# A diffusion trunk in split precision: high and low value features of one neighbourhood head side by side in one product, and new duration estimates for the planner

## The chip, the cores and the metric

The kernel runs on one core of one Trainium2 chip. The metric is the device time of one execution in microseconds (us). Before the change three runs took 1600.81, 1604.31 and 1604.71 us; the median is 1604.31 us.

Engine names are those of the profile: PE is TensorE (PEld its weight loads), DVE is VectorE, ACT is ScalarE, POOL is GpSimd, SP is SyncE, which issues the DMAs.

## The reference

The program is a backbone of two layers over 256 latent tokens and 256 context tokens, width 1024, all in float32. Each layer has four branches side by side, merged by gates, then an MLP with squared ReLU. Cut to what matters here:

```python
u = x * (1.0 + sc1) + sh1
p = split_proj(u @ w_in[l] + b_in[l])            # all branches' inputs and the gates
y_a, y_b = local_branches(p, ...)                # short gated conv | Conformer conv (31 taps, LayerNorm, silu)
y_c = diff_post(diff_latent(q_d, k_d, v_d, k_dc, v_dc, lam), ...)   # differential attention, 4 heads
y_d = na_latent(q_n, k_n, v_n, k_nc, v_nc, rpb)  # neighbourhood attention, 8 heads of 64 features
y = merge_out(p[I_GATE], (y_a, y_b, y_c, y_d), w_branch[l], b_branch[l], w_o[l])
x = layer_norm(ALPHA * x + g1 * y, ...)
x = layer_norm(ALPHA * x + g2 * sq_relu_ffn(x * (1.0 + sc2) + sh2, w_ff1[l], w_ff2[l]), ...)
```

A neighbourhood head is `softmax(q k^T + bias) v`, with 64 features for q, k and v. The latent tokens attend to all 512 tokens, the context tokens (layer 0 alone) to the 256 of the context. In layer 1 the context gives keys and values and nothing else.

## The kernel before

**Precision.** Matrices are multiplied in a rounded float32 format. To keep the accuracy, each operand is split in a high part (rounded by a copy on ACT) and a low part (the rest, a subtraction on DVE). A product of two such operands is three products on PE: high x high, high x low, low x high (`mm3`). The low x low term is left out.

**Weights.** All weights stream through in units of 128 x 1024 numbers (512 KB), in a fixed order: SP loads `raw`, ACT makes `whi`, DVE makes `wlo`, each with three buffers, and PE uses them. In layer 0 a unit of the projections is 24 products over 512 columns (latent and context tokens), in layer 1 mostly 24 over 256 columns.

**Order of a layer.** `main` issues, one after the other: the Conformer branch's inputs, differential attention's first half, the short conv, the second half, merge 0, the first half of the neighbourhood heads (`na_stage` 0), merge 2, the second half (`na_stage` 1), merge 1, merge 3, the output projection, the MLP. Merge i multiplies branch i's output (`ya`, `yb`, `yc`, `yd` for i = 0 to 3) by its weights (tile `br`) and applies the gates; it starts when all four tiles of that branch are there. `yb` comes from the Conformer branch: 31 taps per channel tile on DVE (tile `conf`), then a normalisation over the channels (`mu`, `var`, `rs`), then the splits into `yb`. `yd` comes from the neighbourhood heads.

**A neighbourhood head.** Four or two score tiles `S` on PE, the bias, maximum, exponential and division on DVE and ACT (tile `P`), transposes on PE (`PT`), the split into `pt`, and the products with the values in `na_head` and `pv` (lines 1252 to 1260 and 1289 to 1313). The values of the branch lie in four pairs of tiles, high and low, each 128 keys x 512 features. `pv` takes 128 features, those of two heads, as the stationary operand and 256 queries as the moving one, with three products per 128 keys; the head then reads only its own 64 rows of the PSUM tile `o`. Layer 0 has 6 key tiles per head (4 for the latent, 2 for the context queries) and layer 1 has 4. The 64 rows are split straight from PSUM into `yd`. Differential heads use `pv` with all 128 rows.

**What sets the order.** Each engine's queue is written by a planner in the program (`Sched`). Threads (one per tile, head, weight stream) yield operations with an estimated duration; at each step the planner takes the operation that could start first by these estimates, and among equals the one with the lowest priority number (weights 3, norm 8, projections' evacuation 10 to 12, modulation sums 12, heads 15, softmax 16, `main`'s products 50, taps 90). The estimates thus decide only the order on each engine, buffers' turns and DMA issues included; on the chip the engines wait for one another by semaphores. `gemm` and `score_mm` count a product as its columns at 0.4167 ns plus 2 ns, ACT's operations cost 95 ns plus 0.833 ns per element, 93 more for a per-partition scale, a bias and an accumulator each.

Of the kernel before, what the change touches and what calls it, by code (L numbers as in the profile page):

```python
# [9 lines left out]
F32 = mybir.dt.float32  # L10
F32R = mybir.dt.float32r
AF = mybir.ActivationFunctionType
ALU = mybir.AluOpType
# [12 lines left out]
FIRST = 5  # L26
ADA_PACE = 108
TO_PE = 300.0
PRIO_ADA = 27
PRIO_X = 60  # L30
COLD = 6800.0
# [16 lines left out]
KD = D // 128  # L48
# [101 lines left out]
class Sched:  # L150
    @staticmethod
    def lat(a, b):
# [5 lines left out]
        if "PE" in (a, b):  # L158
            return 200.0 if a == "PE" else TO_PE
        return 205.0 if "POOL" in (a, b) else 143.0  # L160
# [138 lines left out]
def size(ap):  # L299
    n = 1  # L300
    for s in ap.shape[1:]:
        n *= s
    return n


class Kernel(Sched):
# [49 lines left out]
    def act(self, out, in_, func, scale=1.0, bias=None, accum=None):  # L356
        nc, a = self.nc, self._a
        kw = {}
        if bias is not None:
            kw["bias"] = a(bias)  # L360
        if accum is not None:
            kw["accum_out"] = a(accum)
        if isinstance(scale, V) or scale != 1.0:
            kw["scale"] = a(scale)
        cost = 95 + 0.833 * size(out.ap) + 93 * (isinstance(scale, V) + isinstance(bias, V)) + 93 * (accum is not None)
        return self._op("ACT", cost,
                        lambda: nc.scalar.activation(out=out.ap, in_=in_.ap, func=func, **kw),  # L367
                        [out] + ([accum] if accum is not None else []), [in_, scale, bias],
                        table=None if func in (AF.Copy, AF.Identity) else int(func == AF.Ln))
# [60 lines left out]
    def gemm(self, out, pairs, cost, first=True, last=True):  # L430

        n = len(pairs)
        step = max(1, int(1300 // (3 * cost)))
        for i in range(0, n, step):
            calls, r = [], []
            for j in range(i, min(n, i + step)):
                a, b = pairs[j]
                calls += self.mm3(out, a, b, first and j == 0, last and j == n - 1)
                r += [a[0], a[1], b[0], b[1]]
            yield self.mm(calls, [out], r, (cost + 2) * len(calls))  # L440

    def wide(self, l, name, nb, which, tiles, a, ws, done):

# [368 lines left out]
    def ada_all(self):  # L812
# [3 lines left out]
        for g in (1, 2):  # L816
            yield from self.ada(0, g, n)
            n += 16
        self.spawn(self.ada_next(), PRIO_ADA)

# [121 lines left out]
    def first_unit(self, i, n):  # L942
        w = yield self.wait("w", i)
        w = Weight(w, 128)
        p = yield self.alloc("ps", "first", name="mm")
        for k in range(KD):
            for s in range(2):
                yield self.wait("uk", 0, 0, s, k // 2)
            a, b = w(k), self.ucut(0, 0, k, 0, n)
            yield self.mm(self.mm3(p[:, 0:n], a, b, k == 0, k == KD - 1), [p], [*a, *b], 3 * (0.4167 * n + 2))  # L950
        self.release(*w.views())
        self.signal("first", i, val=p)

# [188 lines left out]
        yield from self.wide(l, (br,), 0, range(4), range(4), self.u[l, 0], [], done)  # L1142

    def value_split(self, l, br, t, ps, vs, left, uses):
        vb = yield self.wait("vb", l, br)
        f = yield self.s("att", F32, "vf")
        yield self.tt(f, ps, vb, ALU.add)
        self.release(ps)
        yield from self.split(f, *vs[t])
        self.release(f)  # L1150
        left[0] -= 1
        if not left[0]:
            self.release(vb)
            self.shared((br, l), [x for p in vs for x in p], uses)
# [9 lines left out]
    def score_mm(self, S, q, k, m, q0, k0, nk):  # L1164
        qs, ks = slice(q0, q0 + 128), slice(k0, k0 + nk)
        return self.mm([(S.ap, q[m].ap[:, qs], k[m].ap[:, ks], True, False, {}),
                        (S.ap, q[2 + m].ap[:, qs], k[m].ap[:, ks], False, True, {})],
                       [S], [q[m], q[2 + m], k[m]], 2 * (0.4167 * nk + 2))

    def softmax(self, S, sb, nk, p, stv, i):  # L1170
        nc = self.nc
# [80 lines left out]
    def pv(self, o, vs, c0, pts, s):  # L1252
# [6 lines left out]
                          self.cut(pts[kt // 2], (slice(None), slice((kt % 2) * 256, (kt % 2) * 256 + 256)))))  # L1259
        return self.gemm(o, pairs, 107)  # L1260

    def diff_head(self, l, st, j, n):
        h = 2 * st + j
        pts = []
        for s in range(n // 256):
            p = yield from self.p_parts(l, "d", h, s)
            pts.append(p)
        vs = yield self.wait("dv", l)
        o = yield self.alloc("ps", "att", name="o")
        for s in range(n // 256):  # L1270
            yield from self.pv(o[:, s * 256:s * 256 + 256], vs, h * 128, pts[s], s)
            for p in pts[s]:
                self.release(*p)
        self.done("dv", l)
        sq = yield self.s("tmp", F32, "osq")
        yield self.act(sq[:, 0:n], o[:, 0:n], AF.Square)
        ms = yield self.alloc("ps", "att", name="ms")
        yield self.ones_mm(ms[:, 0:n], self.on128, sq[:, 0:n], True, True)
        r = yield from self.rsqrt(ms[:, 0:n], n)
        self.release(ms)  # L1280
        f = sq[:, 0:n]
        yield self.tt(f, o[:, 0:n], r[:, 0:n], ALU.mult)
        self.release(o, r)
        y = yield from self.pair("y", "yc")
        yield from self.split(f, y[0][:, 0:n], y[1][:, 0:n], self.gd[l])
        self.release(sq)
        self.signal("y", l, 2, h, val=y)

    def na_head(self, l, st, h, n):
        j, e = (h % 4) // 2, h % 2  # L1290
        rows = slice(64 * e, 64 * e + 64)
        pts = []
        for s in range(n // 256):
            p = yield from self.p_parts(l, "n", h, s)
            pts.append(p)
        vs = yield self.wait("nv", l)
        o = yield self.alloc("ps", "att", name="o")
        for s in range(n // 256):
            yield from self.pv(o[:, s * 256:s * 256 + 256], vs, (2 * st + j) * 128, pts[s], s)
            for p in pts[s]:  # L1300
                self.release(*p)
        self.done("nv", l)
        key = ("yd", l, st, j)
        if key not in self.uses:
            self.uses[key] = 0
            y = yield from self.pair("y", "yd")
            self.signal("ydt", l, st, j, val=y)
        y = yield self.wait("ydt", l, st, j)
        yield from self.split(o[rows, 0:n], y[0][rows, 0:n], y[1][rows, 0:n])
        self.release(o)  # L1310
        self.uses[key] += 1
        if self.uses[key] == 2:
            self.signal("y", l, 3, 2 * st + j, val=y)
# [260 lines left out]
    def ff1_rows(self, l, ms, n):  # L1574

        ps, ws = [], []
        for m in ms:
            w = yield from self.weight(l, "f1", m)
            p = yield self.alloc("ps", "main", name="mm")
            ps.append(p)  # L1580
            ws.append(w)
        for k in range(KD):
            yield self.wait("uk", l, 1, 0, k // 2)
            for p, w in zip(ps, ws):
                a, b = w(k), self.ucut(l, 1, k, 0, n)
                yield self.mm(self.mm3(p[:, 0:n], a, b, k == 0, k == KD - 1), [p], [*a, *b], 3 * (0.4167 * n + 2))
        for m, p, w in zip(ms, ps, ws):
            self.release(*w.views())
            self.spawn(self.ff1_evac(l, m, n, p), 10)
# [294 lines left out]
```

## Time and profile before

| | |
|---|---|
| median of three runs | 1604.31 us |
| the profiled execution | 1606.23 us |
| its span, first to last instruction | 1604.5 us |
| granted TensorE clock, mean | 0.994 of full speed |
| PE, PEld busy | 98%, 84% |
| DVE, ACT busy | 80%, 55% |
| mean of the DMA traffic | 158 GB/s |

A row of a group reads: line, engine, operation, tile written <- tiles read, shape written <- shape read, count, then busy us, mean ns of one, and the idle time of the engine ahead of these operations with what ended it. Rows of one engine can overlap, since operations are pipelined: the price of one in a full queue is the distance between two starts. Line 421 is the helper that issues all matrix products, 374 the two-operand operations of DVE, 367 those of ACT, 401 DVE's with a scalar and a tensor; so rows are told apart by their tiles.

### The profile page before, as it was taken

To read this page: it belongs to the slowest core of one execution; us is meant where nothing else is said; L and a number is where in the kernel's file an instruction comes from. 1 tells how busy PE (TensorE), PEld (TensorE's weight loads), DVE (VectorE), ACT (ScalarE), POOL (GpSimd) and SP (SyncE) were. 2 spreads that over 40 slices of the span, in tenths; PEclk is the share of its full clock that TensorE was granted. 3 is DMA by queue.
4 is the path that set the end of the run, shared out by engine and by line. 5 is a ranking of instruction groups with operands and counts; after the bars stand their busy time and mean duration, and the time that the engine had idled before them with its cause. 6 is when DMAs were issued, how large, how long until landed. Compare 5 with 4: busy or idle time off the path is not lost. (4 is left out here: it accounts for less than half of the span.)

```text
span 1604.5 us, 23073 instructions
## 1 busy us (share of the span) xinstructions
PE 1571.9 (98%) x8768; PEld 1349.3 (84%) x8768; DVE 1290.1 (80%) x2156; ACT 883.2 (55%) x1413; POOL 12.0 (1%) x51
## 2 busy tenths in 40 slices
PE   7999999999999999999999999999999989999997
PEld 4888888888888888887887878989998989989997
DVE  3899999699999647986777786999999886774566
ACT  3476376455745544642424334776686585476553
POOL 0000000000000000000000000000000000000000
PEclk9999999999999999999999999999999999999999
DMA  9322322454465155455655644533443335745563
GB/s 373 104 77 79 105 79 79 162 171 160 145 195 160 67 170 197 142 193 177 198 194 192 214 152 141 200 129 136 154 148 116 138 118 176 245 140 189 194 223 108
DMA packets 80707, 254.30 MB, mean 158 GB/s; under 512 B 9028, under 2 KB 13892, under 8 KB 80596
## 3 DMA queue, kind: packets, MB, share of 16 engines
q1 hardware_dynamic: 80596, 252.84, 46.3%
q8 instruction: 68, 1.11, 0.3%
q14 instruction: 43, 0.35, 0.1%
HBM read 250.67 MB, written 2.13 MB: 158 GB/s over the span
## 5 line engine op out<-in xcount | busy, mean ns | idle before, releaser
L421 PE MATMUL mm<-u,whi 128*128 128x512 f32 (+1 forms) x3168 | 786.7, 339 | 1.5 <-DVE u L374 1.0
L421 PEld LDWEIGHTS mm<-u,whi 128*128 128x128 f32 x3168 | 544.9, 190 | 67.7 <-DVE u L374 2.9
L374 DVE TENSOR_TENSOR wlo<-raw,whi 128x1024 fp32r<-128x1024 f32 x335 | 408.5, 1221 | 159.4 <-PE mm L421 70.2
L421 PE MATMUL mm<-u,wlo 128*128 128x512 f32 (+1 forms) x1584 | 534.5, 337 | 0.4 <-DVE wlo L374 0.4
L367 ACT ACTIVATE whi<-raw 128x1024 fp32r<-128x1024 f32 x335 | 353.8, 1057 | 306.5 <-DVE wlo L374 117.6
L421 PEld LDWEIGHTS mm<-u,wlo 128*128 128x128 f32 x1584 | 301.4, 190 | 32.3 <-DVE wlo L374 0.6
L421 PE MATMUL f<-whi,a 128*128 128x512 f32 (+1 forms) x760 | 235.3, 388 | 0.0
L401 DVE SCALAR_TENSOR_TENSOR sums<-araw,cs,sums 128x512 f32<-128x512 f32 x280 | 196.7, 744 | 39.7 <-DMA araw<-in_w_ada 39.4
L421 PEld LDWEIGHTS f<-whi,a 128*128 128x128 f32 x760 | 142.3, 188 | 29.5 <-issue 0.8
L421 PE MATMUL f<-wlo,a 128*128 128x512 f32 (+1 forms) x380 | 147.2, 387 | 0.0
L401 DVE SCALAR_TENSOR_TENSOR conf<-glu,sm,conf 128x512 f32<-128x512 f32 (+1 forms) x240 | 139.0, 611 | 1.1
L421 PEld LDWEIGHTS f<-wlo,a 128*128 128x128 f32 x380 | 71.4, 188 | 14.5 <-DVE wlo L374 0.2
L367 ACT ACTIVATE P<-S,st 128x512 f32<-128x512 f32 (+1 forms) x96 | 58.4, 612 | 11.2 <-DVE st L1173 10.5
L367 ACT ACTIVATE gth<-mm,hb 128x512 f32<-128x512 f32 (+1 forms) x64 | 36.9, 577 | 42.5 <-PE mm L421 42.2
L421 PE MATMUL wo<-whi,mg 128*128 128x512 f32 (+1 forms) x184 | 56.3, 382 | 0.0
L1173 DVE TENSOR_REDUCE st<-S 128x1 f32<-128x512 f32 (+1 forms) x96 | 55.2, 590 | 0.8 <-PE S L421 0.6
L367 ACT ACTIVATE qk<-ra 64x512 fp32r<-64x512 f32 (+1 forms) x72 | 41.5, 576 | 18.5 <-DVE ra L374 17.2
L367 ACT ACTIVATE bh<-br,hb 128x512 f32<-128x512 f32 (+1 forms) x64 | 36.4, 573 | 27.0 <-PE br L421 26.9
L367 ACT ACTIVATE a2f<-mm 128x512 f32<-128x512 f32 (+1 forms) x64 | 30.8, 482 | 33.1 <-PE mm L421 33.0
L421 PE MATMUL S<-qk 128*128 128x512 f32 (+1 forms) x192 | 47.8, 369 | 1.0 <-ACT P L367 0.7
L421 PE MATMUL o<-pt,v 128*128 128x256 f32 x360 | 47.3, 285 | 0.1
L421 PEld LDWEIGHTS o<-pt,v 128*128 128x128 f32 x360 | 45.4, 191 | 1.6 <-issue 0.5
(204 smaller groups left out, 1901.1 us busy)
## 6 DMA issues: line engine op xcount, KB each, us to landing
raw<-in_W SPq DMA_DIRECT2D x344, 512.0 KB
araw<-in_w_ada SPq DMA_DIRECT2D x80, 512.0 KB
a<-in_w_ada SPq DMA_DIRECT2D x32, 256.0 KB
bt<-in_rpb SPq DMA_DIRECT2D x32, 128.0 KB
row<-g SPq DMA_DIRECT2D x12, 256.0 KB
x<-in_x_t SPq DMA_DIRECT2D x8, 256.0 KB
row<-in_ln_g SPq DMA_DIRECT2D x8, 256.0 KB
row<-in_ln_b SPq DMA_DIRECT2D x8, 256.0 KB
```

The lines of the kernel that those rows point to most:

```text
L367: lambda: nc.scalar.activation(out=out.ap, in_=in_.ap, func=func, **kw),
L374: return self._op(eng, cost, lambda: e.tensor_tensor(out=out.ap, in0=x.ap, in1=y.ap, op=op), [out], [x, y])
L401: return self._op("DVE", cost, lambda: nc.vector.scalar_tensor_tensor(out=out.ap, in0=x.ap, scalar=a(s), in1=y.ap, op0=op0, op1=op1), [out ...
L421: nc.tensor.matmul(out=out, lhsT=x, rhs=y, start=start, stop=stop, **kw)
L1173: yield self.dve(68 + 1.04 * nk, lambda: nc.vector.tensor_reduce(out=mx.ap, in_=S.ap, axis=AX.X, op=ALU.max, negate=True), [mx], [S])
```

## The change

Three things:

1. `value_split` writes the values of the neighbourhood branch in another layout: a tile's 512 columns hold, for each of four heads, 64 high features and 64 low ones. Each value tile is split in two halves of 256 features for that.
2. `na_head` uses a new `pv_head`: the stationary operand is one head's 64 high and 64 low features, and it is multiplied by the high and by the low part of the probabilities, two products per 128 keys. Rows 0 to 63 of `o` then hold the high features' part and rows 64 to 127 the low ones'. ACT copies rows 64 to 127 of `o` into a temporary, DVE adds rows 0 to 63, and the sum is split into `yd`. The low x low term is now in the sum.
3. The planner's estimates: a product is its columns plus `MM` = 13.3 ns; an ACT operation with a per-partition scale or bias costs 65 ns more, once; one that writes 64 partitions costs 13 ns plus 0.23 ns per element more.

```diff
+MM = 13.3
@@ act
-        cost = 95 + 0.833 * size(out.ap) + 93 * (isinstance(scale, V) + isinstance(bias, V)) + 93 * (accum is not None)
+        n = size(out.ap)
+        cost = 95 + 0.833 * n + 93 * (accum is not None)
+        if out.ap.shape[0] == 64:
+            cost += 13 + 0.23 * n
+        elif isinstance(scale, V) or isinstance(bias, V):
+            cost += 65
@@ gemm (and in the same way first_unit, score_mm, ff1_rows)
-            yield self.mm(calls, [out], r, (cost + 2) * len(calls))
+            yield self.mm(calls, [out], r, (cost + MM) * len(calls))
@@ value_split
-        yield from self.split(f, *vs[t])
+        if br == "dv":
+            yield from self.split(f, *vs[t])
+        else:
+            for g in range(2):
+                x = f[:, g * 256:g * 256 + 256].re("p (h d) -> p h d", h=4)
+                o = vs[t][g].re("p (h c d) -> p h c d", h=4, c=2)
+                yield from self.split(x, o[:, :, 0, :], o[:, :, 1, :])
@@ new
+    def pv_head(self, o, v, pts, s, c0):
+        n = 2 * len(pts)
+        for kt in range(n):
+            x = v[2 * (kt + 2 * s)][:, c0:c0 + 128]
+            cols = slice((kt % 2) * 256, (kt % 2) * 256 + 256)
+            ps = [p[:, cols] for p in pts[kt // 2]]
+            yield self.mm([(o.ap, x.ap, p.ap, kt == 0 and i == 0, kt == n - 1 and i == 1, {}) for i, p in enumerate(ps)],
+                          [o], [x, *ps], 2 * (107 + MM))
@@ na_head
-            yield from self.pv(o[:, s * 256:s * 256 + 256], vs, (2 * st + j) * 128, pts[s], s)
+            yield from self.pv_head(o[:, s * 256:s * 256 + 256], vs[st:], pts[s], s, (2 * j + e) * 128)
...
+        t = yield self.s("tmp", F32, "olo")
+        yield self.act(t[0:64, 0:n], o[64:128, 0:n], AF.Copy)
+        f = t[rows, 0:n]
+        yield self.tt(f, o[0:64, 0:n], t[0:64, 0:n], ALU.add)
+        self.release(o)
...
-        yield from self.split(o[rows, 0:n], y[0][rows, 0:n], y[1][rows, 0:n])
-        self.release(o)
+        yield from self.split(f, y[0][rows, 0:n], y[1][rows, 0:n])
+        self.release(t)
```

More of the change, by code (lines that the diff above doesn't have):

```diff
@@ L949, in first_unit @@
             a, b = w(k), self.ucut(0, 0, k, 0, n)
-            yield self.mm(self.mm3(p[:, 0:n], a, b, k == 0, k == KD - 1), [p], [*a, *b], 3 * (0.4167 * n + 2))
+            yield self.mm(self.mm3(p[:, 0:n], a, b, k == 0, k == KD - 1), [p], [*a, *b], 3 * (0.4167 * n + MM))
         self.release(*w.views())
@@ L1167, in score_mm @@
                         (S.ap, q[2 + m].ap[:, qs], k[m].ap[:, ks], False, True, {})],
-                       [S], [q[m], q[2 + m], k[m]], 2 * (0.4167 * nk + 2))
+                       [S], [q[m], q[2 + m], k[m]], 2 * (0.4167 * nk + MM))
     def softmax(self, S, sb, nk, p, stv, i):
@@ L1585, in ff1_rows @@
                 a, b = w(k), self.ucut(l, 1, k, 0, n)
-                yield self.mm(self.mm3(p[:, 0:n], a, b, k == 0, k == KD - 1), [p], [*a, *b], 3 * (0.4167 * n + 2))
+                yield self.mm(self.mm3(p[:, 0:n], a, b, k == 0, k == KD - 1), [p], [*a, *b], 3 * (0.4167 * n + MM))
         for m, p, w in zip(ms, ps, ws):
```

## The prediction

> **What bounds the kernel now.** The page comes first, for what is busy and for the products that the change touches.
>
> ```profile
> span 1604.5 us, 23073 instructions
> PE 1571.9 (98%) x8768; PEld 1349.3 (84%) x8768; DVE 1290.1 (80%) x2156; ACT 883.2 (55%) x1413; POOL 12.0 (1%) x51
> L421 PEld LDWEIGHTS o<-pt,v 128*128 128x128 f32 x360 | 45.4, 191 | 1.6 <-issue 0.5
> L421 PE MATMUL o<-pt,v 128*128 128x256 f32 x360 | 47.3, 285 | 0.1
> ```
>
> TensorE is busy 98% of the span, but its rows overlap, so the 285 ns of one product is not its price. The chain of waits in order of time (start, length, what) gives the price: an unbroken stretch divided by its count.
>
> ```profile
> 1250.99 1.44 PE o L421 x12
> 1466.62 23.03 PE mm L421 x192
> 1489.65 21.79 PE f L421 x96
> ...
> 1291.60 1.36 PE S L421 x6
> 1314.76 0.87 PE PT L481 x8
> ```
>
> A product over 256 columns takes 1.44/12 = 0.120 us, the `o` products too; over 512 columns it takes 21.79/96 = 0.227 us; a transpose 0.109 us. The weight loads (191 ns each) hide inside that spacing. So where TensorE never stops, a product left out is 0.120 us gained. Whether it never stops is asked of the stretches around the neighbourhood heads (columns: window, then the sum, then PE, PEld, DVE, ACT and POOL busy, granted clock, DMA share, GB/s).
>
> ```profile
> 350.00:508.00 158.00, 158.00 (x753) 130.13 (x752) 152.00 (x246) 88.89 (x142) 0.00 (x0) 1.00 0.53 172
> 508.00:543.00 35.00, 34.85 (x237) 30.18 (x236) 30.35 (x62) 23.84 (x51) 0.00 (x0) 1.00 0.24 76
> 1050.00:1250.00 200.00, 199.57 (x1326) 183.10 (x1325) 191.28 (x388) 137.39 (x230) 0.53 (x8) 1.00 0.37 129
> 1296.30:1305.70 9.40, 4.25 (x14) 3.38 (x15) 9.21 (x24) 8.20 (x20) 0.00 (x0) 0.72 0.34 112
> ```
>
> TensorE has no gap in the first three, but VectorE is at 152.0/158 = 96%, 87% and 96% there. The two are nearly level, and in the fourth stretch VectorE wins. The timeline of TensorE shows it:
>
> ```profile
> 1295.99 0.28 PE L421 MATMUL mm<-u,wlo 128*128 128x256 f32 x1
> 1299.35 0.33 PE L481 MATMUL PT<-ident,P 128*128 128x128 f32 x1 [3.08 <-ACT P L367]
> 1301.78 0.90 PE L481 MATMUL PT<-ident,P 128*128 128x128 f32 x3 [2.10 <-ACT P L367]
> ...
> 1305.74 0.56 PE L421 MATMUL br<-yb,whi 128*128 128x256 f32 x1
> ```
>
> Layer 1's next large work is merge 1 (`br<-yb`). It needs the fourth conformer channel, whose last split starts on VectorE at 1305.8 (row further down). Until then TensorE has eight transposes and six score products, 8 x 0.109 + 6 x 0.227 = 2.2 us of work in 9.4 us: 7.2 us are lost.
>
> **The change, part by part.**
>
> *Products.* Per head and 128 keys there were three products over 256 columns, now two. Layer 0 has 8 heads x 6 key tiles, layer 1 has 8 x 4: 48 + 32 = 80 products less, 80 x 0.120 = **9.6 us** of TensorE: 5.8 in layer 0 (0.72 per head), 3.8 in layer 1 (0.48). The Trainium skill (TensorE: Matmul & The Clock Gate, section Back-to-back issue gap) puts the spacing at N/2.4 plus 2.5 ns. The trace has 13 ns over 256/2.4 = 107; by the page the term would be 80 x 109 ns = 8.7 us, and the measured spacing decides.
>
> *Rows added.* Each head gets an ACT copy of 64 rows from PSUM into a temporary and a VectorE addition, ahead of its split. Nearest are the split's own rows, same shape and same source, here the five heads of layer 0 after 508 us and the four of layer 1 before 1296:
>
> ```profile
> L367 ACT ACTIVATE yd<-o x5: 592/593/594, 516.9 to 542.6; 64x512 fp32r<-64x512 f32 x5
> L374 DVE TENSOR_TENSOR yd<-o,yd x5: 675/694/697, 517.5 to 543.2; 64x512 fp32r<-64x512 f32 x5
> ...
> L367 ACT ACTIVATE yd<-o x4: 377/378/379, 1243.0 to 1252.5; 64x256 fp32r<-64x256 f32 x4
> L374 DVE TENSOR_TENSOR yd<-o,yd x4: 408/422/428, 1244.0 to 1252.9; 64x256 fp32r<-64x256 f32 x4
> ```
>
> In a queue VectorE's rows overlap too:
>
> ```profile
> 411.02 0.68 DVE L374 TENSOR_TENSOR conf<-conf,rs 128x512 f32<-128x512 f32 x1
> 411.62 0.68 DVE L374 TENSOR_TENSOR yd<-o,yd 64x512 fp32r<-64x512 f32 x1
> ...
> 1303.17 0.42 DVE L374 TENSOR_TENSOR conf<-conf,rs 128x256 f32<-128x256 f32 x1
> 1303.50 0.42 DVE L374 TENSOR_TENSOR S<-S,bt 128x256 f32<-128x256 f32 x1
> ```
>
> The spacing is 0.60 and 0.33 us: 8 x 0.60 + 8 x 0.33 = 7.5 us of VectorE. ACT gets at most 8 x 0.59 + 8 x 0.38 = 7.8 us; at 55% it hides that, except as latency of each head (about 1.2 us in layer 0: copy, then addition). The PSUM bank of `o` is held as before, for one ACT and one VectorE operation.
>
> *Value tiles.* Four per layer are split in two halves of 256 instead of one of 512. Two at 0.33 for one at 0.60: 0.07 us, 8 x 0.07 = 0.6 us of VectorE, as much again on ACT. The strided output has no row; I bound it by no penalty and by twice the time (8 x 0.6 = 4.8 us, off the path but in the same queue) and take none: the taps on `glu`, whose operands lie in two pieces a row, take as long as the sums on whole rows.
>
> ```profile
> L401 DVE SCALAR_TENSOR_TENSOR sums<-araw,cs,sums 128x512 f32<-128x512 f32 x280 | 196.7, 744 | 39.7 <-DMA araw<-in_w_ada 39.4
> ...
> L401 DVE SCALAR_TENSOR_TENSOR conf<-glu,sm,conf 128x512 f32<-128x512 f32 x120 | 85.3, 745 | 0.7
> ```
>
> VectorE's total: 7.5 + 0.6 = **8.1 us** more, against 9.6 less on TensorE.
>
> *The order.* Every engine's queue is planned again, SP's loads with them. The planner now counts 13.3 ns over the columns per product where it counted 2: 24 x 11.3 = 0.27 us more for a weight unit of 24 products. The chip's spacing agrees with the new figure. The old plan thus packed VectorE as if TensorE were 0.27 us per unit faster, and on the chip VectorE waited that out at the head of its queue:
>
> ```profile
> L374 DVE TENSOR_TENSOR wlo<-raw,whi 128x1024 fp32r<-128x1024 f32 x53 | 64.7, 1221 | 7.3 <-issue 4.5 <-ACT ac L367 1.1 <-ACT bh L367 0.7
> ```
>
> That is layer 1 from 1050 to 1270 us, 7.3/53 = 0.14 us per weight. Behind a waiting `wlo` stand softmax, heads and taps. A plan with the right spacing can put some of them ahead: worth between 0 and 7.3 us here; I take half, 3.6, since not every gap is as long as an operation.
>
> *Junction in layer 0.* Merge 3 needs the last head.
>
> ```profile
> L421 PEld LDWEIGHTS br<-yd,whi x9: 187/188/189, 542.3 to 544.9; 128*128 128x128 f32 x9
> ```
>
> Its products start at 542.3 and the last head's split only at 543.2: heads and TensorE arrive together. Three heads lie before 508, five after. Before: TensorE loses 3 x 0.72 = 2.2 us; VectorE gains 3 x 0.60 + 0.3 = 2.1 and has 158 - 152 = 6 us free: 2.2 come through. After: TensorE needs 35 - 3.6 = 31.4 us, VectorE 30.35 + 5 x 0.60 = 33.4: VectorE ends last, 35 - 33.4 = 1.6 come through. Sum **3.8 us**; bounds 0 (heads wholly paced by VectorE) and 5.8.
>
> *Junction in layer 1.* This is the one row of the fourth channel:
>
> ```profile
> L374 DVE TENSOR_TENSOR yb<-conf,yb x2: 416/421/426, 1302.8 to 1305.8; 128x256 fp32r<-128x256 f32 x2
> ```
>
> Four heads lie before it. TensorE's 1.9 us there only lengthen its wait. VectorE gets 4 x 0.33 + 0.3 = 1.6 us more ahead of the channel and 3.6 back: merge 1 starts 2.0 us earlier. The four heads after it give 4 x 0.48 = 1.9. Sum **3.9 us**; bounds 0.3 (nothing regained: 1.9 - 1.6) and 7.6 (7.3 - 1.6 + 1.9).
>
> *Sum.* 3.8 + 3.9 = 7.7 us. The profiled execution took 1606.23 us (span 1604.5 and 1.7 around it): 1598.5 after. It stood 1.9 above the median of the runs, 1604.31, to which the prediction refers: 1604.3 - 7.7 = **1596.6 us**.
>
> **Rivals.**
>
> *VectorE paces both junctions and nothing is regained.* Gain 0 + 0.3: 1604.0 us. For it: 96% in two stretches. Against it: VectorE's own gaps, 6.0, 4.65 (35 - 30.35) and 8.7 us (200 - 191.28).
>
> *The order pays in full.* 5.8 + 7.6 = 13.4 us: 1590.9. For it: planner and chip now agree on the spacing. Against it: in layer 0 VectorE would have to pass its added work without a trace.
>
> *Slower: the cushion is gone.* The 0.27 us per unit that the old plan wrongly saved was a margin: TensorE always came later than planned, so its operands were there. This is why 350 to 508 shows no gap. Without it every lateness of VectorE reaches TensorE wherever VectorE is above about 95%. Then VectorE sets the pace and its 8.1 us are added: 1612.4. It decides from the point at which VectorE's work per weight unit exceeds TensorE's 24 x 0.120 = 2.88 us (layer 1). Against it: fillers, such as taps and modulation sums, can slide. A stop costs more than its length: in the fourth stretch above the granted clock fell to 0.72, and `br` took 0.56 us. The Trainium skill (same page, section on the HAM clock gate) says that idleness of about 3.4 us halves the clock; the drop agrees. By that rule a second stop of that kind would come on top of 1612.
>
> *The change doesn't do what it says*: the products saved were hidden by something else. Against it: the 0.120 spacing of `o` itself. 1604.3.
>
> **How the numbers follow.** Chances: forecast 0.40, both junctions paced by VectorE 0.20, order in full 0.20, slower 0.17, no effect 0.03. A measurement of this kernel tells about 0.3%, 4.8 us, from no change: faster means below 1599.5, slower above 1609.1. The forecast's own range, 1592 to 1600, lies nearly all below: 0.36 faster, 0.04 same. The paced case: 0.02 faster, 0.16 same, 0.02 slower. In full: 0.20 faster. Slower 0.17; no effect 0.03 same. Sum: 0.58, 0.23, 0.19. The range goes from 1588 (in full, less a stop that vanishes) to 1608; it leaves out the slower case.
>
> **What would show it.** Right: 280 `o` products at 0.120 us; `br<-yd` of layer 0 at about 538.5; the stop before `br<-yb` of layer 1 still there, but ended some 6 us earlier in the span (3.8 + 2.0); VectorE near 1298 us busy; `wlo` waits shorter. Wrong: new gaps of TensorE before `PT`, `S` or `mm` elsewhere (the slower case); a stop in front of `br<-yd` as long as the saving (the paced case); a start of `br<-yb` without a stop (the order in full).

## The result, and the profile after

The changed kernel took 1618.47 us (median of four runs, 1613.89 to 1620.5) beside 1604.51 us for the kernel before on the same chip: a ratio of 1.0087, interval 1.0061 to 1.0114. It is 14 us slower; the prediction was 8 us faster, 1596.6 us with a range from 1588 to 1608.

In the code after the change the helpers have moved down: line 421 is now 427, 374 is 380, 367 is 373, 381 is 387, 401 is 407 (in e1 and e8, further down, 422, 375, 368, 382 and 402). First the busy time of the changed kernel, and the groups of the modulation sums and of the head products.

```profile
span 1618.7 us, 22984 instructions
PE 1573.0 (97%) x8688; PEld 1338.1 (83%) x8688; DVE 1300.3 (80%) x2192; ACT 879.6 (54%) x1425; POOL 12.5 (1%) x51
...
L407 DVE SCALAR_TENSOR_TENSOR sums<-araw,cs,sums 128x512 f32<-128x512 f32 x280 | 195.9, 747 | 57.9 <-DMA araw<-in_w_ada 57.4
L427 PE MATMUL o<-pt,v 128*128 128x256 f32 x280 | 38.7, 286 | 0.6 <-DVE pt L380 0.5
```

The 80 products are gone (360 to 280 of `o`, 8768 to 8688 in all), VectorE has 10.2 us more (8.1 reckoned), ACT is no busier. None of that is large. The row that changed is the idle time ahead of the modulation sums: 57.4 us waiting for the loads of `araw`, where it was 39.4.

Busy shares of TensorE hide most of the loss, since its rows overlap. So I use another measure throughout. For each form of product, take the distance between two starts in an undisturbed stretch (0.120 us over 256 columns, 0.227 over 512, 0.109 for a transpose); the **loss** is what the distances in the trace have beyond that, summed. The loss holds stops, and products that a lower clock slowed. By this measure the products' own time is a count times a spacing, so 80 products less give 9.6 us less, 1521.1 for 1530.7, by construction; what the trace adds is that the `o` products still start 0.120 us apart (the median, as before). The loss rose from 53.0 to 77.0. The loss up to the first product of a step, and what each stretch adds (the last one, 7.6 and 8.6 us to the end, is left out):

| loss in us, from step to step | before | after |
|---|---|---|
| up to merge 2 of layer 0 (`br<-yc`) | 25.4 | 27.3 |
| to merge 1 (`br<-yb`) | +0.6 | +10.5 |
| to merge 3 (`br<-yd`) | +0.7 | +2.5 |
| to the second MLP matrix (`f`) | +3.3 | +5.3 |
| MLP of layer 0, to 1000 us | +5.4 | +14.7 |
| layer 1, to its merge 2 | +1.9 | +7.6 |
| to its merge 1 | +7.4 | +0.4 |
| to its output projection (`wo`) | +0.7 | +0.1 |

Two places carry the difference: layer 0's attention ahead of merge 1 (9.9 us more), and the MLP (9.3 more), where the change alters no operation, only the planned order. In layer 1 many small stops (5.7 more) take the place of the one large stop that the prediction started from (7.0 less). The timeline of TensorE after, ahead of layer 1's merge 1:

```profile
1318.86 0.40 PE L427 MATMUL mm<-u,whi 128*128 128x256 f32 x2
1319.10 0.28 PE L427 MATMUL mm<-u,wlo 128*128 128x256 f32 x1
1319.22 0.40 PE L427 MATMUL br<-yb,whi 128*128 128x256 f32 x2
```

The products follow one another 0.12 us apart; nothing stops here, and merge 1 still starts 13.5 us later than the 1305.7 of before.

**How the MLP loses.** Timeline of VectorE after, with the wait in brackets, and the loads that SyncE issued:

```profile
921.18 0.33 SPq L418 DMA_DIRECT2D araw<-in_w_ada  x1
922.32 0.33 SPq L418 DMA_DIRECT2D raw<-in_W  x1
922.74 0.38 SPq L418 DMA_DIRECT2D araw<-in_w_ada  x1
```

```profile
924.93 2.74 DVE L407 SCALAR_TENSOR_TENSOR sums<-araw,cs,sums 128x512 f32<-128x512 f32 x4 [2.64 <-DMA araw<-in_w_ada]
929.46 2.08 DVE L407 SCALAR_TENSOR_TENSOR sums<-araw,cs,sums 128x512 f32<-128x512 f32 x3 [1.79 <-DMA araw<-in_w_ada]
931.46 1.21 DVE L380 TENSOR_TENSOR wlo<-raw,whi 128x1024 fp32r<-128x1024 f32 x1
```

```profile
930.48 0.61 PE L427 MATMUL f<-whi,a 128*128 128x512 f32 x2
932.72 0.50 PE L427 MATMUL f<-wlo,a 128*128 128x512 f32 x1 [1.63 <-DVE wlo L380]
```

Read from the bottom. TensorE stands 1.63 us for `wlo`. `wlo` stands in VectorE's queue behind modulation sums. These waited 1.79 us at the head of the queue for `araw`, whose load had been issued at 922.74 and was there at 929.46, 6.7 us later; the load issued at 921.18 took 3.75. The planner's figure is 524288/355 = 1.48 us of transfer and 2.1 us to land, 3.6 in all; it counts loads one behind the other, so the third in a row lands 3 x 1.48 + 2.1 = 6.5 us after the first's issue. In the trace it is used 8.3 us after it, 1.8 us later than the plan has it. The Trainium skill (DMA: Bandwidth & Descriptors, section Anatomy of one DMA) gives, for loads that GpSimd issues, 2.0 us plus the bytes at 436 GB/s, for one load an estimate of 3.2 us here. These loads are SyncE's, and the trace's 3.75 and 6.7 us decide.

Over the whole MLP (720 to 1000 us), the waits for the sums' loads and for the sums, before and after (what waits <- what ended it: us in total, times, longest; the first sum of each series is an operation of its own, lines 381 and 387):

```profile
DVE sums L401 <- DMA araw<-in_w_ada: 32.7, 20, 3.2
DVE sums L381 <- DMA araw<-in_w_ada: 9.0, 3, 6.2
PEld ada L421 <- DVE sums L401: 4.3, 5, 2.0
PEld f L421 <- DVE wlo L374: 0.2, 1, 0.2
```

```profile
DVE sums L407 <- DMA araw<-in_w_ada: 48.3, 30, 3.0
DVE sums L387 <- DMA araw<-in_w_ada: 7.3, 3, 4.3
PEld ada L427 <- DVE sums L407: 9.6, 9, 1.7
PEld f L427 <- DVE wlo L380: 3.2, 4, 2.1
```

Late loads are nothing new: before, VectorE waited 41.7 us for them, after 55.6 (both rows together). But before they seldom reached TensorE.

**How layer 0's attention loses.** Here VectorE is full; the windows of the changed kernel (columns as in the prediction):

```profile
350.00:400.00 50.00, 46.31 (x205) 37.16 (x204) 48.19 (x78) 25.44 (x39) 0.00 (x0) 0.97 0.51 170
400.00:450.00 50.00, 47.65 (x239) 38.18 (x238) 45.57 (x82) 34.84 (x61) 0.00 (x0) 0.99 0.46 153
```

and the largest stop in it:

```profile
382.97 0.39 PE L427 MATMUL mm<-u,wlo 128*128 128x512 f32 x1
387.05 2.04 PE L427 MATMUL var<-sum,on 128*128 128x512 f32 x2 [3.69 <-DVE sum L380]
```

TensorE waits 3.69 us for a `sum` that stands in a full queue of VectorE. On VectorE the modulation sums ahead of it wait for their loads only briefly:

```profile
361.30 1.42 DVE L407 SCALAR_TENSOR_TENSOR sums<-araw,cs,sums 128x512 f32<-128x512 f32 x2 [0.87 <-DMA araw<-in_w_ada]
...
374.26 2.08 DVE L407 SCALAR_TENSOR_TENSOR sums<-araw,cs,sums 128x512 f32<-128x512 f32 x3 [0.66 <-DMA araw<-in_w_ada]
```

So what makes VectorE late here can't be read from this trace alone.

### The profile page after: what moved, and what is told of

It is laid out like the page before. It is cut to its first block, busy times and chain, and to the rows that moved or that the text cites. A ratio compares the mean times of both kernels' runs of the same rounds, so it can differ in the third digit from the quotient of the medians.

```text
span 1618.7 us, 22984 instructions
## 1 busy us (share of the span) xinstructions
PE 1573.0 (97%) x8688; PEld 1338.1 (83%) x8688; DVE 1300.3 (80%) x2192; ACT 879.6 (54%) x1425; POOL 12.5 (1%) x51
## 5 line engine op out<-in xcount | busy, mean ns | idle before, releaser
L407 DVE SCALAR_TENSOR_TENSOR sums<-araw,cs,sums 128x512 f32<-128x512 f32 x280 | 195.9, 747 | 57.9 <-DMA araw<-in_w_ada 57.4
L427 PEld LDWEIGHTS f<-wlo,a 128*128 128x128 f32 x380 | 71.4, 188 | 17.2 <-DVE wlo L380 3.2
L373 ACT ACTIVATE qk<-ra 64x512 fp32r<-64x512 f32 (+1 forms) x62 | 35.0, 565 | 24.4 <-DVE ra L380 22.1
L373 ACT ACTIVATE P<-P,st 128x512 f32<-128x512 f32 (+1 forms) x42 | 26.5, 643 | 33.1 <-DVE st L1236 27.8
L380 DVE TENSOR_TENSOR a<-a2f,a 128x512 fp32r<-128x512 f32 (+1 forms) x64 | 35.4, 556 | 10.6 <-ACT a L373 9.9
```

What stands on the lines that cost most here:

```text
L380: return self._op(eng, cost, lambda: e.tensor_tensor(out=out.ap, in0=x.ap, in1=y.ap, op=op), [out], [x, y])
L407: return self._op("DVE", cost, lambda: nc.vector.scalar_tensor_tensor(out=out.ap, in0=x.ap, scalar=a(s), in1=y.ap, op0=op0, op1=op1), [out ...
L427: nc.tensor.matmul(out=out, lhsT=x, rhs=y, start=start, stop=stop, **kw)
```

## The experiments

The theory: **the cushion**, the prediction's slower rival. The old estimate of a product, 2 ns beyond its columns, is 11.3 ns too cheap; it made the planned TensorE faster than the real one, by at most 8768 x 11.3 ns = 99 us over the program. By this theory everything else therefore had time in hand. The rivals: that the heads themselves cost more than they save, and that any other figure gives another order, good or bad by **chance**.

### The change in its parts

Heads and layout with the old estimates; old heads with all the new estimates; the product estimate alone; ACT's alone:

```diff
# e1: after.py with the old estimates
-MM = 13.3
+MM = 2
# e3: before.py with the product estimate only
-            yield self.mm(calls, [out], r, (cost + 2) * len(calls))
+            yield self.mm(calls, [out], r, (cost + 13.3) * len(calls))   # and so in the three other places
# e4: before.py with ACT's new cost lines only; e2: e3 and e4 together
```

> The new heads and value layout with the old duration estimates (2 ns per product, 93 ns per ACT operand). Theory cushion (the exact product estimate took away the planner's margin): faster than before by 3 to 10 us, because the 80 products are gone and the margin is still there. Theory VectorE work (the 8.1 us that the heads add on VectorE set the end): slower by 5 to 15 us, like the change itself. Theory lottery (any new order moves the time by some 10 us either way): no fixed sign.

> The old heads with all the new duration estimates. Theory cushion: slower than before by 10 to 24 us, with stops of TensorE spread over layer 0's 350 to 450 us and the modulation sums of the MLP. Theory VectorE work: within 3 us of before. Theory lottery: no fixed sign.

> The old heads, the old ACT estimates, 13.3 ns per product. Theory cushion: most of the loss of the run with all new estimates, 10 to 20 us slower than before. Theory VectorE work: within 3 us of before. If the ACT estimates are what costs, this run is near before.

> The old heads, 2 ns per product, the new ACT estimates. Theory cushion: within 4 us of before, since TensorE's margin stays. Theory that the new ACT figures are wrong (64-row operations planned too long, scale with bias too short): slower by 4 us or more.

| | median us | ratio to before | interval |
|---|---|---|---|
| heads alone (e1) | 1612.58 | 1.0045 | 1.003 to 1.006 |
| all estimates (e2) | 1629.57 | 1.0155 | 1.0138 to 1.0172 |
| product estimate (e3) | 1622.69 | 1.011 | 1.0095 to 1.0125 |
| ACT estimates (e4) | 1607.77 | 1.0021 | 1.0011 to 1.003 |

Before took 1604.32 us beside them. So the estimates cost 25 us, the product's figure alone 18, and the heads then give 11 back (1629.57 to 1618.47). But with the old estimates the heads cost 8 us: the same 9.6 us less work of the busiest engine is a gain in one plan and a loss in the other. No single theory has both halves. The cushion fits e2, e3 and e4 (e2 lies a little above its 24 us) but missed e1, for which it said 3 to 10 us faster. VectorE's added work fits e1 (5 to 15 us slower) but missed e2 and e3, which it had within 3 us of before. Both halves need an explanation.

By the loss measure e3 loses most in the MLP (17.2 us, 5.4 before) and in layer 1 up to merge 2 (7.5, 1.9 before). Ahead of layer 0's merge 1 it loses no more than before; e2 loses some 5 us more there. So the change's loss in that stretch doesn't come from the product's figure alone.

### Cushion or chance

Three more figures for a product in the kernel before; with e3's they make a ladder.

```diff
-            yield self.mm(calls, [out], r, (cost + 2) * len(calls))
+            yield self.mm(calls, [out], r, (cost + MM) * len(calls))   # MM = 2.3, 7, 20
```

> The same with 2.3 ns per product, hardly another estimate but another order. Theory cushion: within 4 us of before. Theory lottery: a change of 5 to 15 us in either direction.

> The old heads, the old ACT estimates, 7 ns per product (2 in the kernel before, 13.3 measured on the chip; 13.3 alone came out 17.7 us slower). Theory cushion (the shorter the plan makes TensorE, the more margin the other engines have): in between, 4 to 12 us slower than before. Theory lottery (any new order costs or brings some 10 us): no relation to the figure, so as likely as slow as 13.3 or as fast as before.

> The same with 20 ns per product, more than the chip takes. Theory cushion: slower than the run with 13.3, 18 to 35 us over before, since the plan now thinks that TensorE leaves more room than it does. Theory lottery: no relation.

| ns beyond the columns | 2 | 2.3 | 7 | 13.3 | 20 |
|---|---|---|---|---|---|
| ratio to before | 1 | 1.0012 | 1.0051 | 1.011 | 1.0176 |
| interval | | 1.0002 to 1.0021 | 1.0034 to 1.0067 | 1.0095 to 1.0125 | 1.0161 to 1.0191 |

The time rises step by step with the figure, through the true value (13.3) and beyond; each run lies where the cushion theory had it. A mere reshuffle moves it by 0.1%: with 2.3 ns only 542 of VectorE's 2156 instructions keep their place in its queue, against 447 with 13.3 ns. So chance alone is an unlikely cause of this series, and the margin explains it. The series holds for the old heads and the old landing figure; two runs below (e12 and e14) go against it with the new heads. Where the loss sits does change from plan to plan: at 7 ns the MLP alone has 20.3 us (31.1 to 51.4), at 20 ns it has 7.4 and the rest is spread over both layers' branches.

### What the cushion had covered

If it is the loads that land late, a later planned landing should mend the changed kernel.

```diff
-                        [out] if isinstance(out, V) else [], [in_], lag=2100.0)
+                        [out] if isinstance(out, V) else [], [in_], lag=3600.0)   # e15: 4500.0
```

> The changed kernel with 3600 ns in place of 2100 for the time from a transfer's end to its landing in the plan. Theory late loads (with the exact product estimate the loads of the modulation weights come later than planned, VectorE waits for them at the head of its queue and TensorE for VectorE): the loss of TensorE between 715 and 1080 us, 15 us in the changed kernel against 6 before, falls to 8 or less and the time to 1608 to 1613. If VectorE's own lateness without loads is what costs, within 3 us of 1618.5.

> The changed kernel with 4500 ns to landing (1602.9 us with 3600). Theory late loads: VectorE's waits for the modulation weights fall from 12 us to under 6, but these waits no longer reach TensorE, so the time is within 3 us of 1602.9. If margin of any kind is what counts, it falls by another 4 us or more.

It does: 1602.85 us, ratio to before 0.9988 (0.9978 to 0.9998), 15.6 us less than the change as made and 5 us below the range that the theory gave. The waits of e9 for the same stretch of the MLP:

```profile
DVE sums L387 <- DMA araw<-in_w_ada: 12.4, 2, 6.8
DVE sums L407 <- DMA araw<-in_w_ada: 11.9, 5, 2.9
PEld ada L427 <- DVE sums L407: 1.1, 3, 0.4
```

The two rows have gone from 55.6 us to 24.3, though the first sum of a series waits longer than it did (12.4 for 7.3), and no wait of `f` for `wlo` is left. The loss in the MLP falls from 14.7 to 0.5 us, below the 5.4 of before, and ahead of merge 1 in layer 0 from 10.5 to 0.9: that stretch, too, had been late through loads or the order that they set, which the trace of the change alone didn't show. The window of e9 there:

```profile
350.00:400.00 50.00, 50.00 (x233) 41.12 (x232) 49.46 (x83) 25.40 (x42) 0.00 (x0) 1.00 0.59 185
```

With 4500 instead of 3600 the kernel takes 1601.61 us (0.998, 0.9971 to 0.999), as expected: there is little more to be had from this figure. VectorE's waits for these loads in the MLP are 15.1 us in e15 (24.3 in e9), not under 6 as expected, and the loss there is 0.5 us in both: these waits no longer reach TensorE.

The same figure with the old heads and all new estimates (e13), and with the new heads and the old estimates (e14):

> The old heads, all new duration estimates, 3600 ns to landing. Theory late loads: the loss of the estimates alone (24.9 us) falls by 12 to 20 us, to 1605 to 1617 us. What the new heads are worth under this plan is the difference to 1602.9 us: 10 us if the 80 products come through, 3 to 8 if layer 0's last heads hold some back, 0 if VectorE paces both. If the late loads were only an accident of the order with the new heads, this run stays above 1622.

> The new heads, the old estimates, 3600 ns to landing (1612.6 us with 2100). Theory late loads plus margin: with 2 ns per product the loads already land in time by the plan's own error, so the change is within 4 us of 1612.6; its loss sits at the two junctions. If the landing figure helps whatever the products' estimate is, 1597 to 1605.

Old heads with the new estimates: 1611.58 us (1.0043, 1.0028 to 1.0058), 18 less than without the landing figure; its loss in the MLP is 0.5 us, too (18.4 in e2). So the landing figure takes back 18 of the 25 us that the estimates cost. How much of that it would give any plan isn't settled: old heads with old estimates and this figure weren't run, and some of the loss that vanishes from the MLP was there before (5.4 us). 10.9 us of loss between merges 1 and 3 of layer 0 stay, whose cause I didn't pursue. Beside e13 the change as made with the same figure (e9) is 8.7 us faster: in this plan the heads are worth about what was reckoned.

New heads with the old estimates: 1617.24 us (1.0081, 1.0065 to 1.0097), 4.7 *more* than e1 and outside both expectations. The MLP is clean here as well (0.5 us), but the stops ahead of the two merges have grown to 18.5 and 15.0 us. The landing figure alone is no remedy: it frees the MLP in each of these plans, and what sets the rest is another matter. Nor is the cheap product a margin in every plan: with the new heads and this landing figure, 2 ns and the old ACT estimates (e14) are 14 us slower than the exact figures (e9).

### Why the heads alone cost time

In e1 the stretch up to layer 0's merge 3 loses 10.5 us (0.7 before), and the one up to layer 1's merge 1 loses 12.2 (7.4 before). The first of these stretches, before and in e1: the window, then the sums and additions in it.

```profile
506.00:542.40 36.40, 36.25 (x244) 31.35 (x243) 32.35 (x65) 25.04 (x52) 0.00 (x0) 1.00 0.23 74
L401 DVE SCALAR_TENSOR_TENSOR sums<-araw,cs,sums 128x512 f32<-128x512 f32 x2 | 1.5, 736 | 0.0
```

```profile
506.00:545.90 39.90, 35.38 (x203) 28.83 (x203) 37.57 (x73) 27.59 (x56) 0.00 (x0) 0.91 0.26 81
L402 DVE SCALAR_TENSOR_TENSOR sums<-araw,cs,sums 128x512 f32<-128x512 f32 x9 | 6.6, 748 | 0.0
L375 DVE TENSOR_TENSOR olo<-o,olo 64x512 f32<-64x512 f32 x4 | 2.7, 682 | 0.7 <-ACT olo L368 0.6
```

VectorE has 5.2 us more to do here. The rows added are 2.7 us; seven modulation sums more are 5.1; other work, 2.6 us, is no longer in the stretch. VectorE is 94% busy. The sums have priority 12, the heads 15: where both could start, the sum goes first.

The sums are not all of it. Before, 30 products of the projections (`mm`) stand among the heads in the last 20 us ahead of merge 3:

```profile
L421 PE MATMUL mm<-u,whi 128*128 128x512 f32 x20 | 6.4, 401 | 0.0
L421 PE MATMUL mm<-u,wlo 128*128 128x512 f32 x10 | 3.9, 393 | 0.0
```

In e1 there are none; the last starts 23.6 us ahead of the merge. TensorE's stops come there, 10 us and more behind the last sum (516.2), each in front of a head's own transposes and products, with nothing else to fill them.

In layer 1 it is the taps. The taps of the Conformer branch, with the first and last start, before and in e1, and the splits of its channels in e1:

```profile
L401 DVE SCALAR_TENSOR_TENSOR conf<-glu,sm,conf x120: 457/477/486, 1035.4 to 1269.7; 128x256 f32<-128x256 f32 x120
```

```profile
L402 DVE SCALAR_TENSOR_TENSOR conf<-glu,sm,conf x120: 459/479/486, 1041.5 to 1282.6; 128x256 f32<-128x256 f32 x120
L375 DVE TENSOR_TENSOR yb<-conf,yb x4: 410/416/418, 1307.9 to 1319.9; 128x256 fp32r<-128x256 f32 x4
```

Merge 1 starts at 1318.4, 1.5 us ahead of the last split at 1319.9. (So on the chip a merge starts once the tiles of its first products are there; it doesn't need all four.) The taps have the last priority, 90, and the last one starts at 1282.6 (1269.7 before): whatever is added to the heads passes them. So give the taps 17, behind heads and softmax:

```diff
-        self.spawn(self.conv_b_taps(l, ct, n, pad, g), 90)
+        self.spawn(self.conv_b_taps(l, ct, n, pad, g), 17)
```

> The new heads with the old estimates (7.3 us over before, with a stop of 12 us in front of layer 1's merge 1 and one of 10 us in front of layer 0's merge 3), and the Conformer taps at priority 17 in place of 90, just behind softmax. Theory junction (VectorE's queue ahead of the fourth conformer channel sets the start of layer 1's merge 1): that stop falls under 4 us and the kernel ends 6 to 12 us earlier, at 1600 to 1606; the stop in layer 0 stays. If something else ends the stop (DMA, ACT), within 3 us of the run without the edit, 1612.

> The kernel before with the Conformer taps at priority 17 in place of 90. Theory junction: the stop of 7 us in front of layer 1's merge 1 goes, 1595 to 1600 us; the heads' change is then worth what the run with both (1596.6 us) differs from this, some 0 to 4 us. If the 80 products come through in full once that stop is gone, this run is 8 to 10 us slower than the run with both, near 1605.

> New heads, taps at 17, and 0 ns per product over the columns in place of 2. Theory cushion: a little more margin still, so between the run with 2 ns (1596.6 us) and 4 us faster. Theory that the figure 2 was the best for other reasons: slower by 3 us or more.

The heads with the old estimates and this priority (e8) take 1596.64 us (0.9956, 0.9941 to 0.997), 16 us less than e1, where 6 to 12 were expected. Their taps end early, and the stop ahead of merge 1 is gone (0.1 us of loss):

```profile
L402 DVE SCALAR_TENSOR_TENSOR conf<-glu,sm,conf x120: 458/479/490, 1037.6 to 1235.6; 128x256 f32<-128x256 f32 x120
```

But the kernel before with the priority alone (e10) takes 1594.97 us (0.9944, 0.9925 to 0.9964), no slower: the whole gain is the priority's, and the heads are worth nothing in this plan. The stop ahead of layer 0's merge 3 is why: 10.3 us in e8, 0.7 in e10, 9.6 us of TensorE's work saved and as much lost. The 38 us ahead of that merge in e10 and in e8:

```profile
500.70:538.70 38.00, 37.85 (x251) 32.65 (x250) 33.64 (x67) 25.43 (x53) 0.00 (x0) 1.00 0.25 84
```

```profile
506.40:544.40 38.00, 32.91 (x189) 26.08 (x188) 35.72 (x71) 26.00 (x54) 0.00 (x0) 0.96 0.25 82
```

With a product at 0 ns, more cushion still (e12), the heads take 1600.72 us (0.9983, 0.9969 to 0.9996), 4 us more than with 2, against the cushion's expectation: the stop ahead of merge 3 is 13.8 us and there are 3.7 us ahead of merge 1. So more cushion isn't better in each place. Ahead of merge 3 the traces show a part of why: e12 has only two sums in the last 38 us, so the sums alone don't make its stop, but like e8 it has no `mm` product in the last 20. e10, without a stop, has 30. What puts these products earlier in some plans isn't shown.

Last, the sums. They may begin at a given weight unit; four units earlier (e11), or eight in the changed kernel with the landing figure (e16), so that fewer should lie in the heads' way:

```diff
-ADA_PACE0 = 44
+ADA_PACE0 = 40   # e11, on e8;   36 in e16, on e9
```

> New heads, old estimates, taps at 17, and the sums of layer 0's modulation weights start 4 weight units earlier (pace 40 in place of 44). Theory sums (their VectorE work of 0.66 us each, ahead of softmax in priority, holds the last heads of layer 0 back): the stop of 10 us in front of layer 0's merge 3 shrinks by 3 to 8 us, and the time with it, to 1589 to 1594. If the heads' own chain (copy, addition, split) makes that stop, within 2 us of the run without, 1596.6.

> The changed kernel with 3600 ns to landing and the sums of layer 0's modulation weights started 8 weight units earlier (pace 36 in place of 44). Theory sums: the loss of 8 us between merge 1 and merge 3 of layer 0 falls by 3 to 8 us, and the time to 1594 to 1600. If the heads' own chain makes that stop, within 2 us of 1602.9.

e11 takes 1593.94 us (0.9934, 0.9916 to 0.9953), the lowest of all, though not beyond noise from e10 and e16, and its loss ahead of merge 3 is 5.3 us where e8 has 10.3 (the medians differ by 2.7 us, the profiled executions, to which the losses belong, by 7.0). e16 takes 1594.98 us (0.9944, 0.9929 to 0.996), 7.9 less than e9, and the loss there is 2.8 us for 8.2. The 38 us ahead of merge 3 in e16 and in e9:

```profile
503.50:541.50 38.00, 38.00 (x211) 32.87 (x211) 28.81 (x58) 25.39 (x49) 0.00 (x0) 1.00 0.17 56
```

```profile
508.30:546.30 38.00, 32.75 (x204) 26.57 (x203) 35.73 (x70) 28.27 (x57) 0.00 (x0) 1.00 0.24 78
```

By the groups of these windows no modulation sum is left in the first (seven are in the second); VectorE has room, and TensorE runs through. The other filler has moved with them: in the last 20 us e16 has 48 `mm` products and e9 has 6 (24 in e11, none in e8). So earlier sums do shorten the stop, but the runs don't part the room on VectorE from the work left to TensorE.

## Why the prediction was wrong

**The step that failed is "The order".** It asked what a plan with the right spacing could gain, found a wait of VectorE (7.3 us at `wlo`) and took half of it, 3.6, with 0 as the other bound. Measured with the old heads, the estimates cost 25 us (e2), the product's 18 (e3).

It also misread its row. The 7.3 us were called waits for TensorE; by the waits in the same window (1050 to 1270 us) TensorE ended 0.5 of them, and most have no cause that the profile shows ("issue"). Before, then after:

```profile
DVE wlo L374 <- issue: 4.5, 15, 0.6
DVE wlo L374 <- PE mm L421: 0.5, 2, 0.3
```

```profile
DVE wlo L380 <- PE nv L427: 1.0, 1, 1.0
DVE wlo L380 <- ACT whi L373: 1.0, 1, 1.0
```

The waits did become shorter, 2.4 us in all for 7.3, and the gain that the step looked for came: the stretch up to merge 1 of layer 1 lost 0.4 us, not 7.4. What the step left out is the price. Layer 1 lost 5.7 us more ahead of its merge 2, where VectorE's waits had cost next to nothing (TensorE was busy for 199.57 of 200 us there); layer 0 lost 9.9 more ahead of merge 1; and the MLP, which the sum didn't look at though the estimates reorder the whole program, 9.3. The bound "between 0 and 7.3" left out a loss although the rival further on described one.

**Products: right.** 280 of `o` are left, at their spacing: 9.6 us less work for TensorE. What the heads are worth in time depends on the plan: 11 us gained between e2 and the change, 8.7 between e13 and e9, nothing between e10 and e8, 8 us lost in e1.

**Rows added: right in size.** 16 additions, 0.545 us each at the median, and VectorE 10.2 us busier in all. **Value tiles: right.** The strided halves follow one another 0.33 us apart, without the penalty that the working had bounded at twice the time (timeline of VectorE after):

```profile
355.76 1.08 DVE L380 TENSOR_TENSOR v<-vf,v 128x256 fp32r<-128x256 f32 x3
356.76 0.68 DVE L380 TENSOR_TENSOR vf<-nv,vb 128x512 f32<-128x512 f32 x1
```

**Junction in layer 0: wrong.** Gain 3.8, bounds 0 and 5.8; with the old estimates merge 3 starts 3.5 us later instead (545.9 against 542.4). The sum took the work that VectorE had in those 35 us and added the new rows. It didn't ask what else the planner would put there, or take away; seven modulation sums came, the `mm` products went, and as with the order, no loss had been allowed for. **Junction in layer 1: wrong** in the same way: heads alone moved the last split from 1305.8 to 1319.9, 14.1 us later, where the sum without the order's 3.6 us has 1.6 us later. 6.1 of them were there at merge 2 of layer 1 already (1241.7 against 1235.6); the rest came with the taps, which give way to everything.

**The rivals.** "The cushion is gone" (0.17, 1612.4 us) named the mechanism of the estimates' part, and the ladder of figures bears it out. Its price was wrong, and so was the carrier: it let VectorE's added 8.1 us through, while the runs show loads that land late, even in the MLP, where VectorE has time (29.93 of 50 us after). That e1 came out at 1612.58 us is luck: there the cheap product figure was kept. The window in the MLP:

```profile
950.00:1000.00 50.00, 47.85 (x207) 35.76 (x206) 29.93 (x44) 20.41 (x28) 0.00 (x0) 1.00 0.32 111
```

Against it the text had said that fillers such as taps and sums can slide. They did, into the heads' way. The page of before had the hint: 39.4 us of idle time ahead of the sums, put down to loads. I quoted that row for the price of a tap and passed over its last column.

**What would show it.** The text called for a stop ahead of merge 1 of layer 1 to stay, and for the slower case new gaps of TensorE elsewhere. The stop went and the gaps came. The text had a start of merge 1 without a stop as a sign of the order's full gain; it came with a slower kernel, so a single place doesn't tell these cases apart. `wlo` waits shorter, a sign of being right, misled in the same way.

**What stays open.** ACT's estimates cost 3.4 us (e4), and I didn't look into how. The 10.9 us of e13 and the spread loss at 20 ns aren't traced to a cause. That late loads make VectorE's queue late ahead of layer 0's merge 1 follows from e9 alone, which moved every load, not from a row. The landing figure on the kernel before wasn't run, nor was a plan that keeps `mm` products back for the last heads.

## What to carry to other kernels

In a planner of this kind a figure that is too cheap for one engine can be a margin for the others; in the old plan it was, in others (e12, e14) it wasn't. Before one is corrected, look at which waits of the others are already late without harm (here 39.4 us of an off-path engine for its loads), and correct those figures in the same step. And price saved work at the place where the engines meet, by asking what the planner will move there: here fillers with a better priority than the heads (the sums) came into their way, and fillers of the busiest engine (the `mm` products) were spent before them.

## What the runs showed of the hardware

A load of 512 KB that SyncE issued behind two others within 1.6 us was used 6.7 us after its issue, the first of the three 3.75 us after; two more loads were issued right behind the three, from 923.17 us on. And a stop costs clock as well as time: in the stretch of e1 with 4.5 us of gaps the granted clock was 0.91, in the same stretch before, without gaps, 1.00. Over 39.9 us that is, as an estimate, 0.09 x 39.9 = 3.6 us of the 10.5 lost there.
